# A time-mixing kernel: six batches transposed by three crossbar DMAs a group from overlapping rows, in place of one DMA a group in token order

## Chip, cores and metric

The kernel runs on one core of one Trainium2 chip. The metric is the device time of one execution in microseconds; the median of three runs of the kernel before is 199.16 us (198.97 to 199.38). The profile is of one execution more, and its times are counted from the start of that execution's span.

## The reference, cut to what matters

```python
x_prev[:, 1:, :] = x[:, :-1, :]                   # x: 16 batches x 2048 tokens x 256
xv = x * time_mix_v + x_prev * (1 - time_mix_v)
xr = x * time_mix_r + x_prev * (1 - time_mix_r)
v = xv @ value_weight
r = xr @ receptance_weight
out = (sigmoid(r) * v) @ output_weight            # float32, 16 x 2048 x 256
```

The key projection of the reference has no part in the output, and the kernel does not compute it.

## The kernel before

**Work on the engines.** The 32,768 tokens are cut into 64 units of 512 tokens, four a batch. The projections want the 256 channels on the partitions, so every batch of `x` is first transposed to bf16, as tile `xt`. The mix weights are folded into the projection weights, so that one mixed operand is `x + c * x_prev`: a scale of the previous tokens by `c` (`scale` L354 on DVE, `scale_pool` L364 on POOL, `scale_act` L652 on ACT) and an add of the tokens themselves (`add` L376 on DVE). Then PE does per unit four matmuls for r and four for v (`project`, L384), ACT the sigmoid of r (L672), DVE the product `z` with v (L711), PE eight matmuls with `z` as the stationary operand (`out_matmuls`, L416), and ACT the copy of that result to SBUF (L471). SP stores pairs of units, 1 MB each (`store`, L437), and at the end smaller pieces.

**Three ways to `xt`.** Batches 0 and 1 are transposed by PE unit by unit; batches 2 to 9 by PE from a tile in which partition p holds tokens 16p to 16p + 15. Their `xt` is in the *slot layout*: 17 slots of 128 columns, where column p of slot j + 1 is token 16p + j, and slot 0 holds slot 16 shifted by one column. A unit reads four slots for its tokens, and the same slots less one for the previous tokens (`tokens`, `slots`). Batches 10 to 15 take no PE transposes. POOL's DMAs (`load`, L162 and L158) cast them from float32 to bf16 into a DRAM tile `x_natural`, two groups of three batches, each batch behind 16 rows of zeros; then a crossbar DMA transpose on SP's queue (`by_dma`, L254) writes the group's `xt_both`. One DMA takes the whole group: 6192 rows (three times 16 + 2048) of 256 elements become 128 partitions of 2 x 6192 elements, in token order. A unit of batches 10 to 14 (`STAGED_PAIRS`) then picks runs of four columns out of 1024 consecutive tokens; a unit of batch 15 takes 512 consecutive tokens, and both give `z` an order of its own, which `out_matmuls` undoes by reading every second or fourth column.

**What sets the order around the change.** The program order is written out by hand, loop by loop (one loop a unit). The first group's transpose stands in the loop of unit 27, the second's in that of unit 39 (`T_AT`). Each waits by an added dependency until the last load of its group has landed, so that it does not run beside a load; the loads of batches 13 to 15 (`STAGE_AT`: loops 33 to 35, on POOL's queue) wait in turn for the first group's transpose. The stores of some units are held back so that SP's queue is free: `FIRST` sends two or one of them ahead of a transpose, `WAITING` sends two, then four, right behind it. SP's queue is served in order. The outputs lie in eleven buffers of 1 MB (seven `o_sb`, later also four `x_bf`), so stores may run late by some units without holding ACT.

Of the kernel before, what the change touches and what calls it, by code (L numbers as in the profile page):

```python
# [9 lines left out]
BF16 = mybir.dt.bfloat16  # L10
# [5 lines left out]
def kernel(  # L16
# [25 lines left out]
    nc = tc.nc  # L42

    B, S, D = x.shape
    P = 128
    KO = D // P
    J = S // P
    UJ = 4
    TU = UJ * P
# [5 lines left out]
    H = UJ // 2  # L55
# [7 lines left out]
    WAITING = {23: 27, 25: 27, 29: 39, 31: 39, 33: 39, 35: 39}  # L63
    ZEROS_AT = 12
    SINGLE = NU - 6
    STAGED_PAIRS = range(STAGED, B - 1)
    STAGE_AT = {33: 13, 34: 14, 35: 15}
    GROUPS = [(2, 3), (4, 5, 6), (7, 8, 9), (10, 11, 12), (13, 14, 15)]
    HALVED = (12, 15)
# [140 lines left out]
    def new_xt(b):  # L210
        if b >= BYUNIT:
            for group in GROUPS:
                if b != group[0]:
                    continue
                if b >= STAGED:
                    t = xtpool.tile([P, KO, len(group) * (PAD + S)], BF16, name="xt_both")
                    for k in range(len(group)):
                        xt[b + k] = t[:, :, k * (PAD + S) + PAD - 1 : (k + 1) * (PAD + S)]
                    xt_both[b] = t
                    return  # L220
                xt_both[b] = xtpool.tile([P, J + 1, KO, len(group), P], BF16, name="xt_both")
                for k in range(len(group)):
                    xt[b + k] = xt_both[b][:, :, :, k]
                    nc.gpsimd.memset(xt[b + k][:, 0, :, 0:1], 0.0)
            return
        xt[b] = consts.tile([P, UB * (UJ + 1), KO, P], BF16, name=f"xt_first{b}")
        (nc.vector if b == 0 else nc.gpsimd).memset(xt[b][:, 0, :, 0:1], 0.0)
# [23 lines left out]
    def by_dma(b, after):  # L251

        new_xt(b)
        op = nc.sync.dma_start_transpose(  # L254
            out=xt_both[b], in_=x_both[b].rearrange("b s d -> (b s) d")
        )
        tc.add_manual_dep(op.ins, after.ins.name, SYNC, reason="not beside a load")
        return op

    def transposes(i):  # L260

# [52 lines left out]
    def slots(piece, off=0):  # L314

        b, _, lo, hi = piece
        j = lo // P + (lo // TU if b < BYUNIT else 0) + off
        return slice(j, j + (hi - lo) // P)

    def by_unit(cols, lo, hi):  # L320

        assert hi - lo in (TU, 2 * TU)
        return cols if hi - lo > TU else cols[:, :, :, lo // TU % 2]

    def tokens(piece, off, ko=None):

        b, _, lo, hi = piece
        if b in STAGED_PAIRS:
            pair = lo // (2 * TU) * 2 * TU + off
            cols = xt[b][:, :, pair : pair + 2 * TU].rearrange("p k (q h i) -> p k q h i", h=2, i=UJ)  # L330
            cols = by_unit(cols, lo, hi)
            return cols if ko is None else cols[:, ko]
        if b < STAGED:
            cols = xt[b][:, slots(piece, off)]
        else:
            cols = xt[b][:, :, off + lo : off + hi].rearrange("p k (j c) -> p j k c", c=P)
        return cols if ko is None else cols[:, :, ko]

    def mixed(piece, ko=None):
        b, m, lo, hi = piece  # L340
        cols = mix[(b * S + lo) // (2 * TU)][:, m]
        if b in STAGED_PAIRS:
            cols = cols.rearrange("p j k c -> p (j k c)")
            cols = cols.rearrange("p (h k q i) -> p k q h i", h=2, k=KO, i=UJ)
            cols = by_unit(cols, lo, hi)
            return cols if ko is None else cols[:, ko]
        j = lo // P % (2 * UJ)
        cols = cols[:, j : j + (hi - lo) // P]
        return cols if ko is None else cols[:, :, ko]
# [53 lines left out]
                stop=(n == len(parts) - 1),  # L403
            )

    def out_matmuls(ps, z, b, jj, n, whole=False):

        if whole:
            slot = z.rearrange("p k (c j) -> p k j c", j=UJ)[:, :, jj : jj + n]
        else:  # L410
            cols = z[:, :, jj * P : (jj + n) * P]
            order = "p k (j c) -> p k j c" if b < STAGED else "p k (c j) -> p k j c"
            slot = cols.rearrange(order, j=n)
        for j in range(n):
            for ko in range(KO):
                nc.tensor.matmul(  # L416
                    out=ps[:, j, :],
                    lhsT=slot[:, ko, j],
                    rhs=wo_bf[:, ko, :],
                    start=(ko == 0),  # L420
                    stop=(ko == KO - 1),
                )

    def store(queue, b, lo, hi, after=None):
        src = o_sb[b, lo // (2 * UJ)]
        j = lo % (2 * UJ)
        src = src[:, j : j + hi - lo, :]
        if b < STAGED:
            dst = out[b].rearrange("(p j) d -> p j d", p=P)[:, lo:hi, :]
        elif b in STAGED_PAIRS:  # L430
            h = lo // (2 * UJ)
            dst = out[b, h * 2 * TU : (h + 1) * 2 * TU].rearrange("(p j) d -> p j d", p=P)[:, j : j + hi - lo]
        else:
            n = min(hi - lo, UJ)
            dst = out[b, lo * P : hi * P].rearrange("(e p j) d -> p e j d", p=P, j=n)
            src = src.rearrange("p (e j) d -> p e j d", j=n)
        op = queue.dma_start(out=dst, in_=src)  # L437
        if after is not None:
            tc.add_manual_dep(op.ins, after.ins.name, SYNC, reason="in turn with the last load")
# [16 lines left out]
    def output(g, z):  # L456
        b, e = divmod(g, UB)
        if e % 2 == 0:
            new_o(b, e // 2)
        o = o_sb[b, e // 2]  # L460
        j0 = e % 2 * UJ
        if g >= NU - 4:
            for h in range(2):
                ps = ps_t_pool.tile([P, H, D], FP32, name="ps_t")
                out_matmuls(ps, z, b, h * H, H, whole=True)
                nc.scalar.copy(out=o[:, j0 + h * H : j0 + (h + 1) * H, :], in_=ps)
            store(nc.sync, b, e * UJ, (e + 1) * UJ)
            return
        ps = ps_o_pool.tile([P, UJ, D], FP32, name="psum_o")
        out_matmuls(ps, z, b, 0, UJ)  # L470
        nc.scalar.copy(out=o[:, j0 : j0 + UJ, :], in_=ps)  # L471
        if b < BYUNIT:
            if e % 2 == 1:
                nc.sync.dma_start(
                    out=unit_rows(out, b, e - 1, 2), in_=o.rearrange("p (e j) d -> p e j d", j=UJ)
                )
        elif g >= SINGLE:
            store(nc.sync, b, e * UJ, (e + 1) * UJ)
        elif e % 2 == 1:
            pair = (b, (e - 1) * UJ, (e + 1) * UJ)  # L480
            if g in FIRST:
                firsts.setdefault(FIRST[g], []).append(pair)
            elif g in WAITING:
                kept.setdefault(WAITING[g], []).append(pair)
            else:
                store(nc.sync, *pair)
# [276 lines left out]
```

## Time and profile before

| | us |
|---|---|
| median of three runs | 199.16 |
| span of the profiled execution, first to last instruction | 197.1 |
| PE busy | 191.8 (97%) |
| DVE busy | 183.2 (93%) |
| ACT busy | 177.2 (90%) |
| POOL busy | 85.9 (44%) |
| first group's transpose: issued, landed 19.0 later | 95.12 |
| second group's transpose: issued, landed 15.2 later | 133.82 |
| last store issued | 193.77 |

The median of the runs is 2.06 us above the span of the profiled execution: what lies ahead of the first and behind the last instruction is not in the span. A row of the windows view gives a stretch, the busy time of each engine in it with the number of instructions, the granted clock of PE, the share of the 16 DMA engines' time that was in use (packets overlap, so a share can be over 1), and GB/s. A row of a timeline gives the start, the length, the engine, the line, the instruction and, in brackets, how long the engine was idle before and what ended that.

### The profile page before, as it was taken

To read this page: it belongs to the slowest core of one execution; us is meant where nothing else is said; L and a number is where in the kernel's file an instruction comes from. 1 tells how busy PE (TensorE), PEld (TensorE's weight loads), DVE (VectorE), ACT (ScalarE), POOL (GpSimd) and SP (SyncE) were. 2 spreads that over 40 slices of the span, in tenths; PEclk is the share of its full clock that TensorE was granted. 3 is DMA by queue.
4 is the path that set the end of the run, shared out by engine and by line. 5 is a ranking of instruction groups with operands and counts; after the bars stand their busy time and mean duration, and the time that the engine had idled before them with its cause. 6 is when DMAs were issued, how large, how long until landed. Compare 5 with 4: busy or idle time off the path is not lost.

```text
span 197.1 us, 3735 instructions
## 1 busy us (share of the span) xinstructions
PE 191.8 (97%) x1358; PEld 123.3 (63%) x1364; DVE 183.2 (93%) x286; ACT 177.2 (90%) x197; POOL 85.9 (44%) x117
## 2 busy tenths in 40 slices
PE   8999999999999999999999999999999999999992
PEld 3556676666666666666666666666666666666660
DVE  0999999999999999999999999999999999999962
ACT  3799899999999999999999999999999999999982
POOL 2745542443665635624334266444443444444200
PEclk9999999999999999999999999999999999999999
DMA  5999999999999999999999999999999999999875
GB/s 171 244 190 223 218 263 253 248 264 259 300 419 278 289 294 336 271 236 206 367 206 290 330 347 191 204 210 284 290 301 424 421 419 419 411 422 421 338 321 219
DMA packets 35465, 58.13 MB, mean 295 GB/s; under 512 B 26004, under 2 KB 27000, under 8 KB 30712
## 3 DMA queue, kind: packets, MB, share of 16 engines
q1 hardware_dynamic: 31792, 41.34, 59.8%
q0 software_dynamic: 3504, 16.44, 41.6%
q8 instruction: 10, 0.16, 0.3%
q10 hardware_dynamic: 152, 0.13, 0.2%
q14 instruction: 7, 0.06, 0.1%
HBM read 34.34 MB, written 39.90 MB: 377 GB/s over the span
## 4 chain that ended last, share of the span: by engine, by line
PE 93%; DMA 4%; issue 0%; SPq 0%; ACT 0%
PE psum_r L384 28%; PE psum_v L384 27%; PE psum_o L416 27%; PE ps_t L272 9%; DMA x_bf<-in_x_dram 2%; DMA w_f<-n_receptance_weight_dram 2%; PE ps_t L416 1%; SPq L174 0%; PE psum_v L416 0%; PE ps_t L384 0%; PE psum_r L416 0%; ACT x_bf L446 0%
## 5 line engine op out<-in xcount | busy, mean ns | idle before, releaser
L364 POOL TENSOR_SCALAR mix<-xt_both,c_sb 128x1024 bf16<-128x1024 bf16 (+1 forms) x55 | 61.1, 1110 | 85.6 <-DVE mix L376 82.4
L711 DVE TENSOR_TENSOR z_sb<-s_sb,psum_v 128x1024 bf16<-128x1024 bf16 (+1 forms) x64 | 76.7, 1200 | 2.2 <-PE psum_v L384 1.1
L376 DVE TENSOR_TENSOR mix<-mix,xt_both 128x1024 bf16<-128x1024 bf16 x112 | 76.8, 696 | 1.4
L384 PEld LDWEIGHTS <-w_bf 128*128 128x128 bf16 x512 | 48.5, 98 | 39.1 <-DVE mix L376 0.4
L672 ACT ACTIVATE s_sb<-psum_r 128x1024 bf16<-128x1024 f32 x63 | 65.3, 1036 | 6.2 <-PE psum_r L384 6.0
L384 PE MATMUL psum_v<-mix,w_bf 128*128 128x512 bf16 (+1 forms) x252 | 64.8, 378 | 0.2
L384 PE MATMUL psum_r<-mix,w_bf 128*128 128x512 bf16 x250 | 64.6, 379 | 0.2
L416 PE MATMUL psum_o<-wo_bf,z_sb 128*128 128x256 bf16 x486 | 63.2, 273 | 0.0
L416 PEld LDWEIGHTS <-z_sb 128*128 128x128 bf16 x512 | 51.9, 103 | 17.9 <-DVE z_sb L510 0.7
L471 ACT COPY o_sb<-psum_o 128x1024 f32<-128x1024 f32 x50 | 51.2, 1024 | 4.9 <-PE psum_o L416 4.9
L289 ACT COPY xt_both<-ps_t 128x1024 bf16<-128x1024 bf16 x32 | 32.9, 1039 | 0.0
L272 PEld LDWEIGHTS <-x_bf 128*128 128x128 bf16 x304 | 19.7, 98 | 8.6 <-DMA x_bf<-in_x_dram 1.1
L272 PE MATMUL ps_t<-ident,x_bf 128*128 128x128 bf16 x304 | 22.5, 219 | 0.3 <-DMA x_bf<-in_x_dram 0.3
L354 DVE TENSOR_SCALAR mix<-xt_both,c_sb 128x1024 bf16<-128x1024 bf16 (+1 forms) x47 | 21.3, 463 | 0.0
L652 ACT ACTIVATE mix<-xt_both,c_sb 128x1024 bf16<-128x1024 bf16 x14 | 16.3, 1163 | 0.0
L376 DVE TENSOR_TENSOR mix<-mix,xt_first 128x1024 bf16<-128x1024 bf16 x15 | 10.6, 714 | 0.1
L471 ACT COPY x_bf<-psum_o 128x1024 f32<-128x1024 f32 x10 | 10.2, 1016 | 0.0
L354 DVE TENSOR_SCALAR mix<-xt_first,c_sb 128x512 bf16<-128x512 bf16 x22 | 6.6, 352 | 0.2
L289 ACT COPY xt_first<-ps_t 128x1024 bf16<-128x1024 bf16 x6 | 6.1, 1042 | 0.2 <-PE ps_t L272 0.2
L557 POOL COPY xt_first<-xt_first 128x254 bf16<-128x254 bf16 x5 | 2.0, 392 | 7.2 <-DVE mix L376 5.7
L364 POOL TENSOR_SCALAR mix<-xt_first,c_sb 128x512 bf16<-128x512 bf16 x6 | 4.1, 685 | 1.5 <-DVE mix L376 1.0
L162 POOL DMA_DIRECT2D x_bf<-in_x_dram x8 | 4.7, 583 | 0.0
(68 smaller groups left out, 52.6 us busy)
## 6 DMA issues: line engine op xcount, KB each, us to landing
out_dram<-o_sb SPq DMA_DIRECT2D x25, 1024.0 KB, 11.6
x_bf<-in_x_dram POOLq DMA_DIRECT2D x8, 1024.0 KB, 14.8
x_natural<-in_x_dram POOLq DMA_DIRECT2D x4, 1024.0 KB, 11.8
out_dram<-x_bf SPq DMA_DIRECT2D x4, 1024.0 KB, 14.4
x_natural<-in_x_dram POOLq DMA_DIRECT2D x4, 512.0 KB, 12.6
out_dram<-x_bf SPq DMA_DIRECT2D x4, 512.0 KB, 4.2
x_bf<-in_x_dram POOLq DMA_DIRECT2D x6, 256.0 KB, 6.5
o_sb<-in_x_dram SPq DMA_DIRECT2D x4, 256.0 KB, 3.8
```

The costliest lines, as they stand in the source:

```text
L162: return nc.gpsimd.dma_start(out=x_bf[b], in_=rows(b), max_dma_last_dim=run)
L272: nc.tensor.transpose(out=ps[:, jj], in_=src[:, jj, ko * P : (ko + 1) * P], identity=idn)
L289: nc.scalar.copy(out=xt[b][:, j0 : j0 + UJ], in_=ps)
L354: nc.vector.tensor_scalar(out=mixed(piece, ko), in0=tokens(piece, 0, ko), scalar1=c_sb[:, m, ko : ko + 1], scalar2=None, op0=ALU.mult,)
L364: op = nc.gpsimd.tensor_scalar(out=mixed(piece, 1), in0=tokens(piece, 0, 1), scalar1=c_sb[:, m, 1:2], scalar2=1.0, op0=ALU.mult, op1=ALU.mult,
L376: return nc.vector.tensor_tensor(out=mixed(piece), in0=mixed(piece), in1=tokens(piece, 1), op=ALU.add)
L384: nc.tensor.matmul(out=ps[:, mo, :], lhsT=w_bf[:, m, ko, mo * P : (mo + 1) * P], rhs=mixed((b, m, e * TU + lo, e * TU + hi), ko), start=(k ...
L416: nc.tensor.matmul(out=ps[:, j, :], lhsT=slot[:, ko, j], rhs=wo_bf[:, ko, :], start=(ko == 0), stop=(ko == KO - 1),)
L471: nc.scalar.copy(out=o[:, j0 : j0 + UJ, :], in_=ps)
L652: nc.scalar.activation(out=mixed(piece, ko), in_=tokens(piece, 0, ko), func=ACT.Copy, scale=c_sb[:, m, ko : ko + 1],)
L672: nc.scalar.activation(out=s_sb, in_=ps_r, func=ACT.Sigmoid)
L711: nc.vector.tensor_tensor(out=z_sb[:, :, c : c + n], in0=s_sb[:, :, c : c + n], in1=ps_v[:, :, c : c + n], op=ALU.mult,)
```

## The change

For batches 10 to 15 the transposed tile now has the slot layout of batches 2 to 9. `by_dma` issues three transposes a group, one a batch. Each reads 128 rows of 4352 elements (17 tokens of 256) that start 16 tokens apart, so that neighbouring rows overlap by one token; the first token of the first row is the last row of zeros. Column group by column group they fill the 34 blocks of 128 columns (17 slots x 2 halves of the channels) of one batch. Slot 0 comes out shifted by the transpose itself. Token order, the four-column runs and the strided reads of `z` are gone, and the stores of all batches address the output as partition p, tokens 16p to 16p + 15.

```diff
@@ new_xt
-                if b >= STAGED:
-                    t = xtpool.tile([P, KO, len(group) * (PAD + S)], BF16, name="xt_both")
-                    for k in range(len(group)):
-                        xt[b + k] = t[:, :, k * (PAD + S) + PAD - 1 : (k + 1) * (PAD + S)]
-                    xt_both[b] = t
-                    return
                 xt_both[b] = xtpool.tile([P, J + 1, KO, len(group), P], BF16, name="xt_both")
                 for k in range(len(group)):
                     xt[b + k] = xt_both[b][:, :, :, k]
-                    nc.gpsimd.memset(xt[b + k][:, 0, :, 0:1], 0.0)
+                    if b < STAGED:
+                        nc.gpsimd.memset(xt[b + k][:, 0, :, 0:1], 0.0)
@@ by_dma
         new_xt(b)
-        op = nc.sync.dma_start_transpose(
-            out=xt_both[b], in_=x_both[b].rearrange("b s d -> (b s) d")
-        )
-        tc.add_manual_dep(op.ins, after.ins.name, SYNC, reason="not beside a load")
+        for k in range(len(next(group for group in GROUPS if group[0] == b))):
+            op = nc.sync.dma_start_transpose(
+                out=xt[b + k].rearrange("p j k c -> p (j k) c"), in_=shifted_rows(b, k)
+            )
+            tc.add_manual_dep(op.ins, after.ins.name, SYNC, reason="not beside a load")
         return op
+
+    def shifted_rows(b, k):
+
+        first = x_both[b][k, PAD - 1 : PAD - 1 + S].rearrange("(p j) d -> p (j d)", p=P)
+        steps = [list(step) for step in first.ap]
+        steps[-1][1] += D
+        return bass.AP(tensor=first.tensor, offset=first.offset, ap=steps)
@@ tokens
-        if b in STAGED_PAIRS:
-            pair = lo // (2 * TU) * 2 * TU + off
-            cols = xt[b][:, :, pair : pair + 2 * TU].rearrange("p k (q h i) -> p k q h i", h=2, i=UJ)
-            cols = by_unit(cols, lo, hi)
-            return cols if ko is None else cols[:, ko]
-        if b < STAGED:
-            cols = xt[b][:, slots(piece, off)]
-        else:
-            cols = xt[b][:, :, off + lo : off + hi].rearrange("p k (j c) -> p j k c", c=P)
+        cols = xt[b][:, slots(piece, off)]
...
@@ out_matmuls
-        if whole:
-            slot = z.rearrange("p k (c j) -> p k j c", j=UJ)[:, :, jj : jj + n]
-        else:
-            cols = z[:, :, jj * P : (jj + n) * P]
-            order = "p k (j c) -> p k j c" if b < STAGED else "p k (c j) -> p k j c"
-            slot = cols.rearrange(order, j=n)
+        slot = z[:, :, jj * P : (jj + n) * P].rearrange("p k (j c) -> p k j c", j=n)
@@ store
-        if b < STAGED:
-            dst = out[b].rearrange("(p j) d -> p j d", p=P)[:, lo:hi, :]
-        elif b in STAGED_PAIRS:
-            h = lo // (2 * UJ)
-            dst = out[b, h * 2 * TU : (h + 1) * 2 * TU].rearrange("(p j) d -> p j d", p=P)[:, j : j + hi - lo]
-        else:
-            n = min(hi - lo, UJ)
-            dst = out[b, lo * P : hi * P].rearrange("(e p j) d -> p e j d", p=P, j=n)
-            src = src.rearrange("p (e j) d -> p e j d", j=n)
+        dst = out[b].rearrange("(p j) d -> p j d", p=P)[:, lo:hi, :]
```

On SP's queue, from the last stores ahead of the first group's transpose to the first behind the second's, before (`o_sb` and `xt_both` numbers tell the buffers apart; DMAHW are the completions of DMAs of SP and ACT, DMASW those of POOL's):

```order
L437 DMA out_0_dram<-o_sb_1171 128x2048 [waits DMAHW2_49,Activation_49]
L254 DMA_TRANSPOSE xt_both_1401<-x_natural_136 128x2x6192 [waits DMASW5_49,DMASW1_49,DMASW6_49,DMASW0_49,DMAHW3_49,DVE_49,Pool_49]
L437 DMA out_0_dram<-o_sb_1255 128x2048 [waits DMAHW4_49,Activation_49]
L437 DMA out_0_dram<-o_sb_1333 128x2048 [waits DMAHW5_49,Activation_49]
L437 DMA out_0_dram<-o_sb_1416 128x2048 [waits DMAHW6_49,DMASW3_49,Activation_49]
L254 DMA_TRANSPOSE xt_both_1805<-x_natural_137 128x2x6192 [waits DMASW2_49,DMASW1_49,DMASW4_49,DVE_49,DMAHW7_49,Activation_49,Pool_49]
L437 DMA out_0_dram<-o_sb_1494 128x2048 [waits DMAHW0_49]
```

The same place now:

```order
L408 DMA out_0_dram<-o_sb_1171 128x2048 [waits DMAHW2_49,Activation_49]
L249 DMA_TRANSPOSE xt_both_1401<-x_natural_136 128x34x128 [waits DMASW5_49,DMASW0_49,DMAHW3_49,DVE_49,Pool_49]
L249 DMA_TRANSPOSE xt_both_1401<-x_natural_136 128x34x128 [waits DMAHW4_49,DMASW6_49]
L249 DMA_TRANSPOSE xt_both_1401<-x_natural_136 128x34x128 [waits DMAHW5_49,DMASW1_49]
L408 DMA out_0_dram<-o_sb_1255 128x2048 [waits DMAHW6_49,Activation_49]
L408 DMA out_0_dram<-o_sb_1333 128x2048 [waits DMAHW7_49,Activation_49]
L408 DMA out_0_dram<-o_sb_1418 128x2048 [waits DMAHW0_49,DMASW3_49,Activation_49]
L249 DMA_TRANSPOSE xt_both_1807<-x_natural_137 128x34x128 [waits DMASW2_49,DMASW1_49,DMASW4_49,DVE_49,DMAHW1_49,Activation_49,Pool_49]
L249 DMA_TRANSPOSE xt_both_1807<-x_natural_137 128x34x128 [waits DMAHW2_49,DMASW2_49]
L249 DMA_TRANSPOSE xt_both_1807<-x_natural_137 128x34x128 [waits DMAHW3_49]
L408 DMA out_0_dram<-o_sb_1496 128x2048 [waits DMAHW4_49]
```

Each transpose became three, one behind the other; the stores around them stand where they stood.

On POOL, the scales near the program's end, where the second group's tile is first read, before (each `mix` number is one pair of units, and two pairs make a batch):

```order
L364 TENSOR_SCALAR mix_201<-xt_both_1401,c_sb_134 128x128x2x4 [waits DVE_49]
L364 TENSOR_SCALAR mix_202<-xt_both_1805,c_sb_134 128x128x2x4 [waits DMAHW7_49,DVE_49,PE_49]
L364 TENSOR_SCALAR mix_202<-xt_both_1805,c_sb_134 128x128x2x4 [waits DVE_49]
L364 TENSOR_SCALAR mix_203<-xt_both_1805,c_sb_134 128x128x2x4 [waits DVE_49,PE_49]
L364 TENSOR_SCALAR mix_203<-xt_both_1805,c_sb_134 128x128x2x4 [waits DVE_49]
L364 TENSOR_SCALAR mix_204<-xt_both_1805,c_sb_134 128x128x2x4 [waits DVE_49,PE_49]
L364 TENSOR_SCALAR mix_204<-xt_both_1805,c_sb_134 128x128x2x4 [waits DVE_49]
L364 TENSOR_SCALAR mix_205<-xt_both_1805,c_sb_134 128x128x2x4 [waits DVE_49,PE_49]
L364 TENSOR_SCALAR mix_205<-xt_both_1805,c_sb_134 128x128x2x4 [waits DVE_49]
L364 TENSOR_SCALAR mix_206<-xt_both_1805,c_sb_134 128x8x128 [waits DVE_49,PE_49]
```

And now:

```order
L348 TENSOR_SCALAR mix_201<-xt_both_1401,c_sb_134 128x8x128 [waits DVE_49]
L348 TENSOR_SCALAR mix_202<-xt_both_1807,c_sb_134 128x8x128 [waits DMAHW1_49,DVE_49,PE_49]
L348 TENSOR_SCALAR mix_202<-xt_both_1807,c_sb_134 128x8x128 [waits DVE_49]
L348 TENSOR_SCALAR mix_203<-xt_both_1807,c_sb_134 128x8x128 [waits DVE_49,PE_49]
L348 TENSOR_SCALAR mix_203<-xt_both_1807,c_sb_134 128x8x128 [waits DVE_49]
L348 TENSOR_SCALAR mix_204<-xt_both_1807,c_sb_134 128x8x128 [waits DMAHW2_49,DVE_49,PE_49]
L348 TENSOR_SCALAR mix_204<-xt_both_1807,c_sb_134 128x8x128 [waits DVE_49]
L348 TENSOR_SCALAR mix_205<-xt_both_1807,c_sb_134 128x8x128 [waits DVE_49,PE_49]
L348 TENSOR_SCALAR mix_205<-xt_both_1807,c_sb_134 128x8x128 [waits DVE_49]
L348 TENSOR_SCALAR mix_206<-xt_both_1807,c_sb_134 128x8x128 [waits DMAHW3_49,DVE_49,PE_49]
```

The scales stand in the same order with another shape, and where the first scale of the group waited for the group's one DMA, the first scale of each batch now waits for that batch's own. On PE no instruction moved.

More of the change, by code (lines that the diff above doesn't have):

```diff
@@ L65 @@
     SINGLE = NU - 6
-    STAGED_PAIRS = range(STAGED, B - 1)
     STAGE_AT = {33: 13, 34: 14, 35: 15}
@@ L318, in slots @@
         return slice(j, j + (hi - lo) // P)
-    def by_unit(cols, lo, hi):
-        assert hi - lo in (TU, 2 * TU)
-        return cols if hi - lo > TU else cols[:, :, :, lo // TU % 2]
     def tokens(piece, off, ko=None):
         b, _, lo, hi = piece
-        if b in STAGED_PAIRS:
-            pair = lo // (2 * TU) * 2 * TU + off
-            cols = xt[b][:, :, pair : pair + 2 * TU].rearrange("p k (q h i) -> p k q h i", h=2, i=UJ)
-            cols = by_unit(cols, lo, hi)
-            return cols if ko is None else cols[:, ko]
-        if b < STAGED:
-            cols = xt[b][:, slots(piece, off)]
-        else:
-            cols = xt[b][:, :, off + lo : off + hi].rearrange("p k (j c) -> p j k c", c=P)
+        cols = xt[b][:, slots(piece, off)]
         return cols if ko is None else cols[:, :, ko]
@@ L341, in mixed @@
         cols = mix[(b * S + lo) // (2 * TU)][:, m]
[L342 to L346, printed above, removed]
         j = lo // P % (2 * UJ)
@@ L404, in project_unmixed, with out_matmuls @@
             )
-    def out_matmuls(ps, z, b, jj, n, whole=False):
-        if whole:
-            slot = z.rearrange("p k (c j) -> p k j c", j=UJ)[:, :, jj : jj + n]
-        else:
-            cols = z[:, :, jj * P : (jj + n) * P]
-            order = "p k (j c) -> p k j c" if b < STAGED else "p k (c j) -> p k j c"
-            slot = cols.rearrange(order, j=n)
+    def out_matmuls(ps, z, b, jj, n):
+        slot = z[:, :, jj * P : (jj + n) * P].rearrange("p k (j c) -> p k j c", j=n)
         for j in range(n):
@@ L464, in output @@
                 ps = ps_t_pool.tile([P, H, D], FP32, name="ps_t")
-                out_matmuls(ps, z, b, h * H, H, whole=True)
+                out_matmuls(ps, z, b, h * H, H)
                 nc.scalar.copy(out=o[:, j0 + h * H : j0 + (h + 1) * H, :], in_=ps)
```

## The prediction

> **What bounds the kernel now.** I read the page first, then the windows by stage, then SP's and POOL's timelines, then the DMA traffic around one transpose. The page, with the span, the engines' busy time and the chain that ended last:
>
> ```profile
> span 197.1 us, 3735 instructions
> PE 191.8 (97%) x1358; PEld 123.3 (63%) x1364; DVE 183.2 (93%) x286; ACT 177.2 (90%) x197; POOL 85.9 (44%) x117
> PE 93%; DMA 4%; issue 0%; SPq 0%; ACT 0%
> ```
>
> PE carries the chain. How much it idles between its first transpose and the last unit is in the windows (the heading names the columns; the last two numbers are the share of the DMA engines and GB/s):
>
> ```profile
> core 0: us, PE busy (x) PEld busy (x) DVE busy (x) ACT busy (x) POOL busy (x), PEclk, DMA share, GB/s
> 10.25:190.30 180.05, 179.69 (x1296) 116.56 (x1303) 176.17 (x263) 168.50 (x181) 80.92 (x102) 1.00 1.05 302
> 112.00:117.00 5.00, 5.00 (x33) 2.90 (x31) 4.90 (x8) 4.80 (x6) 2.46 (x3) 1.00 0.95 390
> 118.00:133.00 15.00, 14.95 (x94) 9.15 (x94) 14.97 (x21) 13.72 (x15) 7.76 (x8) 1.00 1.03 204
> 138.00:147.00 9.00, 8.89 (x55) 5.57 (x56) 8.98 (x14) 8.18 (x9) 3.47 (x4) 1.00 1.27 290
> 148.00:186.00 38.00, 37.84 (x235) 24.36 (x236) 37.87 (x52) 35.13 (x38) 16.20 (x15) 1.00 1.01 417
> 186.00:191.00 5.00, 5.00 (x37) 3.49 (x36) 3.73 (x6) 4.27 (x8) 0.00 (x0) 1.00 0.62 252
> 191.00:194.50 3.50, 2.33 (x18) 1.21 (x15) 1.87 (x4) 2.33 (x5) 0.00 (x0) 1.00 0.86 332
> ```
>
> In 180.05 us PE idles 180.05 - 179.69 = 0.36 us, at a granted clock of 1.00. So nothing that makes DVE, ACT or POOL faster can bring more than some tenths. The second thing to see is the last column but one. From 118 us on the DMA engines are full in every stage: loads (118 to 133), the second group's transpose (138 to 147), the backlog of stores (148 to 186). Only at 186 us, 5 to 8 us from the end, does the backlog clear. DMA is a second bound that stands just below PE.
>
> **Part one: operands, shapes, order.** The instructions of PE stay as they are; the scales and weight loads get the shape that batches 8 and 9 have already. The groups by shape for 116 to 128 us (slot layout) and then for 134 to 172 us (token order), mean ns of one before the second bar:
>
> ```profile
> L376 DVE TENSOR_TENSOR mix<-mix,xt_both 128x1024 bf16<-128x1024 bf16 x10 | 6.7, 688 | 0.0
> L364 POOL TENSOR_SCALAR mix<-xt_both,c_sb 128x1024 bf16<-128x1024 bf16 x5 | 5.6, 1115 | 5.3 <-DVE mix L376 5.3
> L416 PEld LDWEIGHTS <-z_sb 128*128 128x128 bf16 x40 | 3.9, 98 | 1.5
> ...
> L376 DVE TENSOR_TENSOR mix<-mix,xt_both 128x1024 bf16<-128x1024 bf16 x30 | 20.2, 690 | 0.0
> L364 POOL TENSOR_SCALAR mix<-xt_both,c_sb 128x1024 bf16<-128x1024 bf16 x15 | 16.8, 1122 | 22.0 <-DVE mix L376 20.7 <-PE psum_v L384 1.3
> L416 PEld LDWEIGHTS <-z_sb 128*128 128x128 bf16 x120 | 13.2, 114 | 3.3
> ```
>
> An add costs 690 ns against 688, a POOL scale 1122 against 1115, a weight load of `z` 114 against 98. The 16 ns of 192 weight loads (24 units by 8) are 3.1 us of PEld, but matmuls run over them: PE has no gap for them to fill beyond the 0.36 us. In the tail the weight loads themselves wait for DVE's `z`:
>
> ```profile
> 192.00 0.33 PEld L416 LDWEIGHTS <-z_sb 128*128 128x128 bf16 x4 [0.26 <-DVE z_sb L510]
> ```
> Gain: 0 to 0.4 us, and I take 0, since it would need all of PE's idle time to be of this kind. The stores of batches 10 to 15 now write pieces 16 KB apart in place of whole megabytes. In the backlog the first stores are of batches 7 to 9, which are written so already, the later ones of batches 10 and up:
>
> ```profile
> 150.00:155.00 5.00, 5.00 (x32) 3.22 (x31) 4.99 (x8) 4.59 (x6) 2.05 (x3) 1.00 1.02 424
> 165.00:170.00 5.00, 5.00 (x33) 3.24 (x32) 4.98 (x8) 4.59 (x6) 2.25 (x2) 1.00 1.01 421
> ```
>
> 424 against 421 GB/s: no price for 8 KB pieces. For the last stores' 1 to 4 KB pieces there is no such row; I take 0, within 0.1 us either way.
>
> **Part two: the transposes.** SP's queue, and the landing of the two transposes:
>
> ```profile
> 95.12 15.38 SPq L254 DMA_TRANSPOSE xt_both<-x_natural  x1
> 110.61 20.99 SPq L437 DMA_DIRECT2D out_dram<-o_sb  x3
> 133.82 12.33 SPq L254 DMA_TRANSPOSE xt_both<-x_natural  x1
> 146.20 3.41 SPq L437 DMA_DIRECT2D out_dram<-o_sb  x4
> ...
> DMA to landing us min/median/max: 15.2/17.1/19.0
> ...
> DMA packets 10200, 2.61 MB, mean 290 GB/s; under 512 B 10200, under 2 KB 10200, under 8 KB 10200
> ```
>
> The last row is the DMA traffic of 138 to 147 us: 10200 packets in 9 us, 256 B each, at 290 GB/s, and nothing else in flight. So the rate is the transpose's own. A group was 6192 rows of 512 B, 3.17 MB: 10.93 us. It becomes 3 x 128 rows of 8704 B, 3.34 MB: 11.52 us at the same rate. **Size: +0.59 us a group, +1.18 us both.**
>
> The two added boundaries in each group have no row in this trace; two neighbours bound them. Traffic of 133 to 149 us in 40 slices of 0.4 us:
>
> ```profile
> GB/s 369 451 430 410 389 311 205 154 116 36 222 291 288 291 291 288 291 291 288 291 291 288 291 291 288 291 291 288 291 291 288 291 291 288 291 291 447 532 389 369
> ```
>
> From stores to a transpose there is a hole: the five slices from 135.4 us lack 85 + 136 + 174 + 254 + 68 = 717 of 290 GB/s each, 0.29 MB, 0.99 us of transposing. From the transpose to stores there is none: SP is done with it at 133.82 + 12.33 = 146.15 us, the store behind is issued at 146.20, and in the slice at 147.4 the one's data give way to the other's. A second transpose behind a first would also be issued some 1.3 us before the first one's data end, and no store packet is left that delays some of the 16 engines more than others. So the boundary is nearest to the row without a hole; but the first data of a transpose may need a little longer than a store's, so below 0 it cannot go. Bounds 0 and 0.99 us, value 0.15, times four: **+0.6 us** (0 to 4.0). Should the 128 short source rows, 8 KB apart, read more slowly, that is a rival below; the value here is the same rate. **Sum: the DMA work between 95 and 149 us grows by 1.18 + 0.6 = 1.8 us.**
>
> **What the 1.8 us are worth.** The DMAs of the two groups form one line: transpose one, loads of batches 13 to 15 (held until it lands), transpose two (held until they land), backlog. What is added is spent where the DMA engines are idle: 5 x 0.05 = 0.25 us at 112 to 117, 5 x 0.38 = 1.9 us at 186 to 191, 3.5 x 0.14 = 0.5 us at 191 to 194.5. Together 2.6 us. 1.8 fit; the last store starts when its copy is done, as before. If the added time is D, the end moves by D - 2.6 where that is positive. It moves by more than 0.2% (0.4 us, about what a measurement of this kernel can tell from no change) from D = 3.0.
>
> **Who waits for a later landing.** POOL's queue:
>
> ```profile
> 113.47 1.12 POOL L364 TENSOR_SCALAR mix<-xt_both,c_sb 128x1024 bf16<-128x1024 bf16 x1 [2.33 <-DVE mix L376]
> 114.64 0.56 POOL L162 DMA_DIRECT2D x_natural<-in_x_dram  x1
> 116.22 1.11 POOL L364 TENSOR_SCALAR mix<-xt_both,c_sb 128x1024 bf16<-128x1024 bf16 x1 [1.02 <-DVE mix L376]
> 123.82 1.12 POOL L364 TENSOR_SCALAR mix<-xt_both,c_sb 128x1024 bf16<-128x1024 bf16 x1 [1.31 <-DVE mix L376]
> 154.99 1.12 POOL L364 TENSOR_SCALAR mix<-xt_both,c_sb 128x1024 bf16<-128x1024 bf16 x1 [1.29 <-PE psum_v L384]
> ```
>
> The load at 114.64 waits for the first group's landing at 95.12 + 19.0 = 114.1 and reached its place at 114.59; the scale behind it idles 1.02 us more. With +0.9 us the group lands at 115.0 and the scale at 116.22 still starts in time; from about +1.5 us it would start late. The first readers of the two groups stand at 123.82 and 154.99, 9.7 and 6.0 us after the landings (the second 133.82 + 15.2 = 149.0). Now each batch waits for its own third, so that slack only grows. The stores behind the transposes leave SP 1 us later; their buffers, eleven for a pair of units each, are due again only several pairs later.
>
> **The rivals.** *A hole at each boundary.* Each of the three transposes starts as the one behind stores did. For it: the only start in the trace has a hole. Against it: there it goes with packets of stores still in flight on some engines. At 0.75 us, D = 1.18 + 3.0 = 4.2, the end 1.6 us later: 200.7; at 0.99, 201.7. It decides from (3.0 - 1.18) / 4 = 0.46 us.
>
> *The short rows read more slowly.* A packet reads 256 B. Before, neighbouring rows lay 512 B apart and 8 KB were read in one piece; now neighbouring rows lie 8 KB apart, and the same row is read again only 128 packets later. For it: the loads show a DMA that moves only 204 GB/s while the engines are full. Against it: the flat 288 to 291 GB/s of the slices look like a pace of the engines, not of the memory. Halfway between 290 and 204, at 247 GB/s, a group takes 13.5 us, D = 2 x 2.6 + 0.6 = 5.8, the end 3.2 us later: 202.3; at 204, some 208. It decides from 275 GB/s.
>
> The Trainium skill, page "DMA: Bandwidth & Descriptors", section "Latency and other measured facts", gives crossbar transposes 350 to 400 GB/s for contiguous sources and 261 with a middle dimension that is not contiguous, a loss of about 30%. This trace has 290 for a contiguous source, so the page's first figure does not hold here; whether its loss does, no run here shows yet. By 261 GB/s as it stands a group would take 12.8 us, D would be 4.4, and the end 200.9 us, by an estimate from that page. The same page's section on crossbar transposes names nothing against sources whose rows overlap.
>
> *POOL held at the load.* If transpose one lands over 3 us late, the scales behind the load come late, DVE's adds after them, and PE idles: over 203 us. It needs one of the two rivals above at its upper end.
>
> *Faster.* PE's idle 0.36 us is all that shorter scales and weight loads could give: 198.8 at best.
>
> **How the numbers follow.** The forecast, absorbed: 0.50, at the median of before, 199.2 (the profiled span of 197.1 plus the 2.06 us outside it). Hole at the boundaries: 0.20, 199.6 to 201.7. Slower reading: 0.20, 199.6 to 208. POOL held: 0.04. Faster: 0.06. The range reaches down to 198.8 and up to 201.4: that leaves out half of the faster case, half of the slower reading, a little of the holes, and POOL held, under 0.2 together. Chances: faster 0.06, same 0.50, slower 0.44.
>
> **What would show it.** Right: the transposes at about 290 GB/s with no dip between three, a group's data over in 11.5 to 12 us, PE idle still under 0.5 us from 10 to 190 us, the backlog clearing near 188 and the DMA share of 186 to 191 nearer to 1. Wrong: dips at the boundaries, a rate under 275, or a DMA share of 1 up to the last store. PE gaps between 115 and 125 us would show POOL held.

## The result, and the profile after

The changed kernel takes 207.46 us (median of four runs, 207.08 to 208.35) against 199.15 us (198.97 to 199.38): a ratio of 1.0417 [1.0378, 1.0457], 8.3 us slower. The forecast was 199.2 us, with a range up to 201.4. Times of traces are those of one profiled execution each; its span was 205.4 us, against 197.1 before. One of the ten runs of number 5 below took 1148.26 us, for a reason not known, and is not in its ratio; every other run counts.

The page, with the span, the engines and the chain that ended last, by engine and then by line:

```profile
span 205.4 us, 3751 instructions
PE 191.9 (93%) x1364; PEld 120.7 (59%) x1364; DVE 183.1 (89%) x286; ACT 177.3 (86%) x197; POOL 86.1 (42%) x117
PE 77%; DMA 6%; DVE 4%; SPq 4%; issue 2%; POOL 2%; ACT 1%; DVEq 0%; POOLq 0%
PE psum_v L368 23%; PE psum_r L368 22%; PE psum_o L395 22%; PE ps_t L274 7%; DMA xt_both<-x_natural 4%; SPq L249 3%; DMA w_f<-n_receptance_weight_dram 2%; DVE mix L360 2%; POOL mix L348 1%; DVE z_sb L682 1%; PE ps_t L395 1%; DVE mix L338 1%; PE psum_r L382 1%; ACT xt_first L284 1%; SPq L173 0%
```

No engine has more to do: PE is busy for 191.9 us, against 191.8. But the transposes stand on the chain now (DMA `xt_both` 4%, SP's queue at L249 3%), and before they did not. The windows, columns as before:

```profile
120.00:125.00 5.00, 3.13 (x20) 1.80 (x19) 4.57 (x7) 3.35 (x4) 4.02 (x6) 1.00 1.04 288
130.00:190.00 60.00, 60.00 (x373) 36.30 (x371) 59.71 (x82) 55.51 (x60) 25.01 (x23) 1.00 1.01 332
186.00:191.00 5.00, 5.00 (x33) 3.05 (x32) 4.97 (x7) 4.77 (x7) 1.12 (x1) 1.00 1.02 421
191.00:196.00 5.00, 4.94 (x37) 3.15 (x35) 3.16 (x7) 4.09 (x9) 0.00 (x0) 1.00 1.01 414
196.00:204.00 8.00, 0.00 (x0) 0.00 (x0) 0.07 (x1) 0.35 (x1) 0.00 (x0) 0.66 0.85 325
```

Two things differ. PE has one hole, 1.9 us between 120 and 125. And the backlog of stores, which cleared at 186 us before (a DMA share of 0.62 at 186 to 191), now fills the DMA engines to the end: 1.02, 1.01, and still 0.85 in the last 8 us, in which PE does nothing. The last copy to SBUF starts at 195.97 us; the last store lands at 204.2, where it landed at 196.1 before.

Where the backlog was delayed is seen in SP's timeline (three merged transposes a row) and in the slices of the DMA traffic, first 97 to 120 us (0.575 us a slice), then 140 to 160 us (0.5 us a slice):

```profile
95.70 20.41 SPq L249 DMA_TRANSPOSE xt_both<-x_natural  x3
116.21 20.53 SPq L408 DMA_DIRECT2D out_dram<-o_sb  x3
140.26 15.34 SPq L249 DMA_TRANSPOSE xt_both<-x_natural  x3
```
```profile
GB/s 427 328 299 256 228 214 147 176 191 154 290 290 288 292 83 158 100 91 121 289 289 290 291 258 74 245 18 83 295 94 5 41 291 291 289 477 442 299 399 456
GB/s 344 148 16 88 141 79 126 260 289 290 291 289 292 105 52 220 198 115 173 291 290 289 292 285 88 124 139 186 280 288 291 290 291 391 419 426 328 492 410 393
```

Between their starts the transposes run at the same flat rate as before, 288 to 292 GB/s, but for one stop in the first group (number 2). Each of the three starts with a dip, though. The second of the second group: 105, 52, 220, 198, 115, 173 lack 877 of 6 x 290, and 877 / 290 x 0.5 us = 1.5 us. By the trace's packets (256 B each, 1133 a microsecond at the steady rate) the data of the first group, from the first packet to the last, take 17.72 us, from 99.92 to 117.64, against 12.37 before (99.72 to 112.09); those of the second 15.59 us, from 141.58 to 157.17, against 12.38 (135.30 to 147.68).

PE's hole comes through POOL. The rows of POOL, DVE and PE:

```profile
118.67 0.56 POOL L161 DMA_DIRECT2D x_natural<-in_x_dram  x1 [3.73 <-DMA xt_both<-x_natural]
119.27 1.13 POOL L348 TENSOR_SCALAR mix<-xt_both,c_sb 128x1024 bf16<-128x1024 bf16 x1
120.43 0.69 DVE L360 TENSOR_TENSOR mix<-mix,xt_both 128x1024 bf16<-128x1024 bf16 x1 [2.22 <-POOL mix L348]
122.30 1.02 PE L368 MATMUL psum_v<-mix,w_bf 128*128 128x512 bf16 x4 [1.87 <-DVE z_sb L682]
```

The load waits for the last of the three landings (118.14 us, against 114.1) and holds POOL's queue; the scale behind it starts at 119.27 instead of 116.22, DVE's add waits 2.22 us for it, and PE 1.87 us for the `z` behind that.

### The profile page after: what moved, and what is told of

It is laid out like the page before. It is cut to its first block, busy times and chain, and to the rows that moved or that the text cites. A ratio compares the mean times of both kernels' runs of the same rounds, so it can differ in the third digit from the quotient of the medians.

```text
span 205.4 us, 3751 instructions
## 1 busy us (share of the span) xinstructions
PE 191.9 (93%) x1364; PEld 120.7 (59%) x1364; DVE 183.1 (89%) x286; ACT 177.3 (86%) x197; POOL 86.1 (42%) x117
## 4 chain that ended last, share of the span: by engine, by line
PE 77%; DMA 6%; DVE 4%; SPq 4%; issue 2%; POOL 2%; ACT 1%; DVEq 0%; POOLq 0%
PE psum_v L368 23%; PE psum_r L368 22%; PE psum_o L395 22%; PE ps_t L274 7%; DMA xt_both<-x_natural 4%; SPq L249 3%; DMA w_f<-n_receptance_weight_dram 2%; DVE mix L360 2%; POOL mix L348 1%; DVE z_sb L682 1%; PE ps_t L395 1%; DVE mix L338 1%; PE psum_r L382 1%; ACT xt_first L284 1%; SPq L173 0%
## 5 line engine op out<-in xcount | busy, mean ns | idle before, releaser
L395 PEld LDWEIGHTS <-z_sb 128*128 128x128 bf16 x512 | 49.8, 98 | 19.7 <-DVE z_sb L481 0.7
```

What stands on the lines that cost most here:

```text
L395: nc.tensor.matmul(out=ps[:, j, :], lhsT=slot[:, ko, j], rhs=wo_bf[:, ko, :], start=(ko == 0), stop=(ko == KO - 1),)
```

## The experiments

Two questions were asked: what lengthens the transposes, and which of the two consequences, the late stores or PE's hole, sets the time. Below, the loss of a transpose or a group is the time of its data less its packets at 1133 a microsecond, so 0 means the steady rate from the first packet to the last; what a start loses is what has been lost by the time the rate is flat. Each ratio is to runs of the kernel before that were made along with the run, with medians of 199.11 to 199.35 us.

**1. Three DMAs a group, in token order (`e1_three_token_order`).** The kernel before, with its one transpose cut into one a batch; rows, layout and bytes stay.

```diff
-        op = nc.sync.dma_start_transpose(
-            out=xt_both[b], in_=x_both[b].rearrange("b s d -> (b s) d")
-        )
+        for k in range(len(next(group for group in GROUPS if group[0] == b))):
+            op = nc.sync.dma_start_transpose(
+                out=xt_both[b][:, :, k * (PAD + S) : (k + 1) * (PAD + S)], in_=x_both[b][k]
+            )
```

> The kernel before with its one transpose a group cut into three, one a batch (2064 rows each), token order and all else as before. Theory S (each crossbar DMA has a slow start of its own, whatever it reads): two more starts a group cost what the changed kernel's profile lost beyond its size, (17.7 - 12.4) + (15.6 - 12.4) = 8.5 us less 1.2 us of size, over four boundaries, some 1.8 us each, so about 7.3 us more DMA work, of which some 2 us are absorbed at the end: 204 to 206 us, with a dip in the 256-byte traffic at each third. Theory R (the short rows 8 KB apart read slowly at first, the number of DMAs does not matter): 199.2 us within 0.4, no dips at the thirds.

Measured: 202.0 us (201.39 to 202.33), ratio 1.0125 [1.008, 1.017]. Traffic at 97 to 120 us, and the last windows:

```profile
GB/s 356 385 242 256 211 183 58 276 290 290 290 291 182 178 183 284 290 287 290 285 143 85 57 288 290 289 291 290 368 427 427 442 442 399 370 413 456 200 57 214
```
```profile
186.00:191.00 5.00, 5.00 (x33) 3.24 (x32) 4.55 (x7) 4.40 (x7) 0.00 (x0) 1.00 1.01 409
191.00:196.00 5.00, 3.15 (x25) 1.94 (x23) 1.86 (x4) 3.01 (x6) 0.00 (x0) 1.00 0.98 382
196.00:204.00 8.00, 0.00 (x0) 0.00 (x0) 0.00 (x0) 0.00 (x0) 0.00 (x0) 0.76 0.08 29
```

Neither theory alone: starting again costs 0.7 to 1.2 us each (182, 178, 183 is the second start, 143, 85, 57 the third), 3.8 us for the four, and the data of the groups take 13.86 and 14.03 us. The time is 2.8 us longer, of the changed kernel's 8.3. The data of the second group end 3.3 us later than before, in the changed kernel 9.5 us. Of the 6.2 us between the two, about 3 are dearer starts (all six counted), 1.2 the size and 1.4 a fetch of instructions (number 2); most of the rest lies between the groups. The span is 2.5 us longer, so only 0.8 us was absorbed in this execution, where the prediction had up to 2.6.

**2. One DMA a group, from the overlapping rows (`e2_one_strided`).** The other part alone: 400 rows (`ROWS`) over all three batches in one transpose. It also transposes rows between the batches (13,600 packets instead of 12,384, 12.00 us at the steady rate), and writes a small block of zeros behind the last batch and one column a batch.

```diff
-        for k in range(len(next(group for group in GROUPS if group[0] == b))):
-            op = nc.sync.dma_start_transpose(
-                out=xt[b + k].rearrange("p j k c -> p (j k) c"), in_=shifted_rows(b, k)
-            )
+        op = nc.sync.dma_start_transpose(
+            out=xt_both[b].rearrange("p j k c -> p (j k) c"), in_=shifted_rows(b)
+        )
...
+        steps[0][1] = ROWS
```

> The changed kernel with one transpose a group over 400 rows 16 tokens apart (386 are needed; the rest are padding rows, zeroed by one small DMA a group), slot layout as in the changed kernel. Size by the 290 GB/s of the trace: 400 x 8704 B = 3.48 MB, 12.0 us against 10.9 before, so 2.1 us more for both. Theory S: one start a group as before, no dips inside, all of the 2.1 us absorbed: 199.0 to 199.8 us. Theory R: the reads are as far apart as in the changed kernel and the slow stretches stay: 205 us or more.

Measured: 202.81 us (202.04 to 204.78), ratio 1.0184 [1.0113, 1.0256]. Neither theory's time came: it lies between the two, and the profiled execution is the slowest of the four. The steady rate from these rows is 289 to 291 GB/s: they are not read more slowly in the run. The one start of each group loses 1.70 and 1.79 us, against 1.20 and 1.34 before. Over all of their data the groups lose 3.06 and 2.71 us (1.44 and 1.45 before), since each has one stop more, which is no start. In the first group it is the last 1.4 us of the data, behind a fetch of 16 KB of instructions at 114.74 us. In the second it stands in the middle of the run. Traffic at 148 to 153 us, 0.125 us a slice, and the queue that stands beside it:

```profile
GB/s 291 287 287 291 291 295 289 293 287 287 289 293 295 289 285 295 287 289 293 350 270 268 274 102 27 12 8 8 8 6 92 289 289 295 289 293 289 289 283 295
q14 instruction: 1, 0.01, 0.5%
```

A fetch of 8 KB of instructions starts at 150.44 us, one packet, and so on one of the 16 DMA engines; 0.4 us later the transpose stands almost still on all of them: 0.9 us lost. The same is found in the changed kernel, at 111 to 119 us (0.2 us a slice), where 16 KB were fetched at 113.60:

```profile
GB/s 20 200 289 262 140 14 4 17 8 93 278 253 355 248 102 14 0 4 9 10 9 101 292 288 297 287 291 287 292 288 297 287 287 684 655 0 655 655 0 655
q8 instruction: 1, 0.02, 0.7%
```

The first stop, from 111.8 us, is the start of the third transpose; the second, from 113.8 to 115.2, lies in the middle of it and loses 1.4 us. In numbers 3, 6 and 9, which also have three transposes a group, a 16 KB fetch falls into the run of the first group's third transpose too, and 1.5 to 1.6 us are lost.

**3. The loads of the second group one unit later (`e3_loads_later`).** The changed kernel; POOL's scale no longer stands behind a load that waits.

```diff
-    STAGE_AT = {33: 13, 34: 14, 35: 15}
+    STAGE_AT = {34: 13, 35: 14, 36: 15}
```

> The changed kernel with the loads of batches 13 to 15 one loop later in the program, so that POOL reaches the first of them when the first group has nearly landed. In the changed kernel's profile POOL sat 3.7 us at that load and PE idled some 1.9 us at 120 to 125 us. Theory D (the end is set by the DMA engines, which are full up to the last store): PE's gap goes or shrinks below 0.5 us and the time stays within 1 us of 207.5. Theory W (the wait on POOL is what the time was lost to): 205.5 us or less.

Measured: 206.94 us (206.15 to 207.26), ratio 1.0387 [1.0337, 1.0437], which can't be told from the changed kernel's [1.0378, 1.0457]. The windows:

```profile
112.00:130.00 18.00, 18.00 (x112) 10.75 (x110) 17.86 (x26) 16.64 (x18) 9.34 (x11) 1.00 1.10 257
191.00:196.00 5.00, 2.81 (x22) 1.63 (x20) 1.86 (x4) 2.80 (x6) 0.00 (x0) 1.00 1.01 413
196.00:204.00 8.00, 0.00 (x0) 0.00 (x0) 0.00 (x0) 0.00 (x0) 0.00 (x0) 0.63 0.73 277
```

PE's hole is gone (18.00 of 18.00 us) and the time stays: the end is set by the stores, and PE's 1.9 us lie beside them.

**4. Six DMAs a group (`e4_six`).** The changed kernel with each transpose cut in two at slot 16: many long and short starts.

```diff
+            for lo, hi in ((0, UB * 2), (UB * 2, J + 1)):
+                op = nc.sync.dma_start_transpose(
+                    out=xt[b + k][:, lo:hi].rearrange("p j k c -> p (j k) c"),
+                    in_=shifted_rows(b, k)[:, lo * D : hi * D],
...
```

> The changed kernel with each batch's transpose cut into two (16 and 18 blocks of 128 columns), six a group, same rows, same bytes. Theory S: six more starts at some 1.8 us each, 11 us more DMA work with nothing left to absorb it, and POOL held longer at its load: 216 to 222 us. Theory R: the same reads in the same order, 207 to 209 us.

Measured: 209.6 us (one run). Neither theory's time came, and the second is nearer. Data of 17.98 and 18.05 us; the twelve starts lose 0.3 to 1.5 us, 0.95 on average. So the count of starts is not all: twice as many add 0.3 and 2.5 us to the groups (1.5 of the 2.5 are a fetch in the run, at 157.57 us), not the 4 to 5 us that three more starts at the changed kernel's price would add. Where DMAs are short (1.8 and 2.0 us of data each at the steady rate), a start costs less. Why was not found out.

**5 and 6. The changed kernel with less to store (`e5_later_less`, `e6_less`).** The four held stores behind the second group's transposes are left out, 4.2 MB of output that is not written; at 417 GB/s that is 10 us of DMA work, more than was added. Number 5 has the later loads of number 3 as well, number 6 has not.

```diff
-            for pair in kept.pop(g, []):
+            for pair in kept.pop(g, []) if g < CROSS else []:
```

> The kernel of the run before last (loads one loop later, no gap of PE left) with the four stores behind the second group's transposes left out: 4.2 MB of output are not written, some 10 us of DMA work at 417 GB/s. Theory D (the end is set by the line of DMA work alone): the line now ends before PE does, and the time is PE's own, 199.0 to 199.8 us. Theory P (something else in the changed kernel, its operands or its stores, slows PE or the tail): over 200.5 us.

> The changed kernel, loads where they were, with the same four stores left out. With the line of DMA work out of the way the wait on POOL should show alone. Theory D: 1.9 us above the run without that wait, 200.9 to 201.8 us. Theory W (the wait on POOL is most of the loss): 204 us or more. If the wait is made up for later: 199.5 us.

Measured: number 5 takes 199.37 us (nine of the ten runs 198.80 to 200.45), ratio 1.0006 [0.9984, 1.0029]; number 6 takes 201.23 us (200.75 to 201.69), ratio 1.0087 [1.0054, 1.0121]. The windows of number 5:

```profile
112.00:130.00 18.00, 18.00 (x112) 10.73 (x111) 17.87 (x26) 16.68 (x18) 9.30 (x11) 1.00 1.08 263
130.00:190.00 60.00, 60.00 (x375) 36.47 (x374) 59.38 (x82) 55.22 (x59) 24.10 (x22) 1.00 1.00 317
186.00:191.00 5.00, 5.00 (x35) 3.16 (x33) 4.25 (x6) 4.27 (x8) 0.00 (x0) 1.00 0.62 247
```

With room in the DMA line and no hole in PE, the changed kernel takes what the kernel before takes: the two together are the whole of the loss. What would only lengthen the line of DMA work, a slower store for instance, number 5 can't show, since it has 10 us less of that work. For this there are the rows of the changed kernel above: its stores of 186 to 196 us, which have the new addresses, move 421 and 414 GB/s, against 417 in the backlog of before. The hole alone is worth 201.23 - 199.37 = 1.9 us. The waits of number 6 at 112 to 130 us (who waited for whom, sum, times, longest) show it as the same chain as in the changed kernel:

```profile
POOL x_natural L161 <- DMA xt_both<-x_natural: 3.3, 1, 3.3
DVE mix L360 <- POOL mix L348: 1.8, 1, 1.8
PE psum_v L368 <- DVE z_sb L682: 1.4, 1, 1.4
```

**7. A store between the transposes (`e7_stores_between`).** The changed kernel, with two of the held stores put between the three transposes. If a start is slow because the transpose before is still draining, ordinary packets could fill it.

```diff
+            if k < 2:
+                store(nc.sync, *between.pop(0))
...
-            last_t = by_dma(T_AT[g], whole)
+            last_t = by_dma(T_AT[g], whole, kept.get(g, []))
```

> The changed kernel with one held store of 1 MB behind the first and one behind the second transpose of each group, in place of all of them behind the third; the same work in another order. Theory F (at a start the DMA engines lack descriptors, and a store's data fill the hole): of four starts at some 1.4 us most are filled, 202 to 204 us. Theory K (a transpose needs all 16 engines in step, and store packets put them out of step, so that a start behind a store costs as much or more): 207 us or above.

Measured: 209.35 us (208.54 to 210.25), ratio 1.0496 [1.0447, 1.0544]. Traffic at 97 to 120 us:

```profile
GB/s 413 342 299 299 232 155 106 132 78 199 289 290 290 290 376 442 328 356 85 199 187 150 232 237 289 289 289 291 401 399 356 328 100 228 202 155 258 261 289 289
```

The store passes at 328 to 442 GB/s, and behind it the transpose starts with the same dip (85, 199, 187, 150, 232, 237: 1.3 us). Less the two stores (2.5 us each at 417 GB/s) the groups lose 5.2 and 5.6 us, 1.7 to 1.9 us a start (with a 16 KB fetch at 142.10 us in the second group's first start). The slow start belongs to the transpose that starts, and a store ahead of it does not make it cheaper. The time by itself would not show this. With the stores in between, the third transpose lands later still, POOL waits 7.5 us at its load, and PE has a hole of 5.6 us:

```profile
112.00:130.00 18.00, 12.40 (x66) 6.65 (x65) 11.60 (x18) 10.27 (x12) 6.58 (x8) 0.81 0.96 215
```

**8. The first transpose one unit later (`e8_before_one_later`).** The kernel before; it was to move the transpose, and the stores held around it, against the instruction fetch.

```diff
-    T_AT = {27: 10, 39: 13}
...
+    T_AT = {28: 10, 39: 13}
...
```

> The kernel before with its first transpose one loop (3 us) later. In its profile a 16 KB fetch of instructions came at 111.84 us, as that transpose's data ended; in four other profiles here one came while a transpose ran, and its 256-byte traffic then fell to a tenth for 1.2 to 1.6 us. Theory I (the fetch stops the transpose): the fetch, at about 112 us, falls into the data, and they take 13.5 to 14.2 us in place of 12.4. Against it: 12.2 to 12.7 us, wherever the fetch falls. In either case the line of DMA work starts some 2 to 3 us later, so 200 to 203 us.

Measured: 200.7 us (one run). The transpose hardly moved (issued at 95.66 us, 95.12 before); the fetch did, to 116.62 us, outside the data. So it doesn't say what it was made for, and why it takes 200.7 us was not found out. It does show a first group without a fetch (11.84 us of data, 0.5 us less than before), and a second with a fetch of 16 KB at 136.46 us, within its start (13.09 us, 0.7 us more).

**9. Rows 8704 B apart (`e9_pitch`).** The changed kernel, with a DRAM tile in which every row of 17 tokens has its own place, so that no rows overlap and they no longer lie 8192 B apart. One more load a batch (64 KB) writes the repeated tokens.

```diff
-        x_both[group[0]] = dpool.tile([len(group), PAD + S, D], BF16, name="x_natural")
+        x_both[group[0]] = dpool.tile([len(group), P + 1, J + 1, D], BF16, name="x_natural")
...
+        return x_both[b][k, :P].rearrange("p j d -> p (j d)")
```

> The changed kernel with its DRAM tile cast into rows of 17 tokens each (8704 B apart, none overlapping) in place of rows 8192 B apart that overlap by one token; the token ahead of each row comes by one small load more a batch, 64 KB. The transposes read the same number of bytes in the same order. In the profiles so far a second or third start cost 1.0 to 1.8 us with rows 8 KB apart (mean 1.4) and 0.7 to 1.2 with whole batches in one piece (mean 0.95). Theory Q (the power-of-two distance makes a start slower): the starts come down to about 0.95 us, some 2.5 us less in both groups, 205 to 206 us with the small loads. Theory N (short rows far apart are slower at a start, whatever the distance): starts of 1.4 us as before, 207 to 209 us.

Measured: 206.1 us (205.82 to 206.95), ratio 1.0362 [1.0335, 1.0389]: by the medians 1.4 us less than the changed kernel, in spite of the added loads, though the intervals overlap a little (1.0378 to 1.0389). Traffic at 138 to 160 us, 0.55 us a slice:

```profile
GB/s 209 216 439 417 357 432 292 160 105 133 288 290 290 290 290 222 85 141 148 289 290 290 290 290 220 107 92 95 290 290 289 290 290 471 275 462 477 372 358 477
```

The starts are shorter: 1.04 to 1.25 us, 1.14 on average over the five without a fetch, between the 0.95 of theory Q and the 1.4 of theory N. So the way the rows lie matters, but this is a part of what the rows of the change cost. The edit changed two things at once, the distance and the overlap; which of them helps is not shown.

**10. The instruction fetch moved (`e10_fetch_earlier`).** The kernel before, with its first warm-up on PE replaced by more and smaller matmuls. PE's program gets longer at its head, and so the fetches of 16 KB come earlier in the work.

```diff
-    warm_up(WARM)
+    ps_warm = ps_t_pool.tile([P, TU], FP32, name="ps_t")
+    for _ in range(48):
+        nc.tensor.matmul(
+            out=ps_warm[:, :64], lhsT=ones, rhs=wide[:, :64], start=True, stop=True
+        )
```

> The kernel before with its first warm-up on PE (six matmuls of 512 columns and one of 128) replaced by 48 matmuls of 64 columns: 82 PE instructions more at the very start. If the 16 KB fetches are PE's, they come some 5 to 6 us earlier against the rest, the one at 111.84 us then in the middle of the first group's data. Theory I (a fetch stops a transpose): those data take 13.5 to 14.2 us in place of 12.4, and the time rises by 0.3 to 1.5 us. Against it: 12.2 to 12.7 us with a fetch in the middle, and the time within 0.5 us of before. Where no fetch falls into the data the run says nothing.

Measured: 199.77 us (199.15 to 200.28, ten runs), ratio 1.0024 [1.0001, 1.0047]. The fetch came at 110.81 us in place of 111.84, one microsecond earlier and not 5 to 6. Traffic at 109 to 114 us, first of the kernel before, then of this one, 0.125 us a slice:

```profile
GB/s 293 291 287 291 287 291 293 293 291 283 295 287 291 293 293 291 283 289 293 291 293 293 1244 18 80 918 0 131 852 66 852 66 328 721 66 852 66 524 524 66
q8 instruction: 1, 0.02, 1.4%
```
```profile
GB/s 285 293 287 291 295 291 283 293 293 287 291 295 291 283 414 274 268 272 41 18 2 0 0 2 8 8 10 8 10 12 254 295 293 289 291 293 287 285 293 295
q8 instruction: 1, 0.02, 1.5%
```

Before, the fetch fell on the moment in which the stores took over. A microsecond earlier it falls into the run, and the transpose stands for 1.4 us; the data of this group take 14.11 us in place of 12.37 (its start, too, loses more, 1.66 us against 1.20). The second group had a 16 KB fetch at 135.14 us, just ahead of its first packet; now its fetches come at 149.08 us, with its last packets, and it takes 12.03 us in place of 12.38. The time moved by only 0.24% [0.01%, 0.47%].

## Why the prediction was wrong

**The step that failed** is the boundary term of part two: 0.15 us, four times, 0.6 us in all, with bounds of 0 and 0.99. Measured, the added starts cost 1.8, 1.6, 1.5 and 1.1 us, 6.0 us in all, above the upper bound of 4.0. (The third of the first group lost 3.0 us, of which some 1.4 are the fetch; the two run into each other.) The reason given was half right. The next transpose was indeed issued before the data of the one ahead ended (109.54 us, flat rate until 110.7), and no store was in flight. But that a hole needs stores in flight was wrong: number 7 shows the same dip behind a store, number 1 behind a transpose. The trace of before had the right row: its start from stores to a transpose, which the prediction measured at 0.99 us and then set aside for the row of the other direction, a transpose giving way to stores. That is another operation's start. The one row of a transpose starting was the one to take. Its 0.99 us lies within the 0.7 to 1.2 that number 1 measured with the rows of before. (Counted by packets this start lost 1.34 us and the first group's 1.20; the slices of the traffic also count bytes of the last stores.) The rival of a hole at each boundary, with a chance of 0.20, had this mechanism; its highest price, 201.7 us, was still too low.

**What was missing** is that the rows of the change make a start dearer. Means of starts without a 16 KB fetch inside: 0.92 us from contiguous tokens (number 1, 0.7 to 1.2), 1.14 from rows 8704 B apart (number 9, 1.04 to 1.25), 1.4 from rows 8192 B apart (the changed kernel and number 3, 1.1 to 1.8; in number 5 one lost 2.15). The groups do overlap: the whole-group starts from contiguous tokens in before and in numbers 8 and 10 lost 0.77 to 1.66 us. Also missing was the fetch of instructions, 1.4 us. Before, the 16 KB fetch of the first group came at 111.84 us, as its data ended, and that of the second at 135.14, just ahead of its first packet; the longer data of the first group reach over the one.

The sum, from the profiled executions, up to the end of the second group's data:

| | predicted, us | measured, us |
|---|---|---|
| first start later | 0 | 0.2 |
| size, both groups | 1.18 | 1.2 |
| four added starts | 0.6 | 6.0 |
| fetch within the first group | – | 1.4 |
| from the first group's data to the second's, longer | 0 | 0.7 |
| D | 1.8 | 9.5 |
| absorbed (D less the end) | 1.8 of up to 2.6 | 1.2 |
| end later | 0 | 8.3 |

**What the D is worth** was right as a rule and wrong in size. Above the slack the end moves with D, and number 5 shows that nothing else moves it but PE's hole. The slack was too large: by the profiled executions 0.8 us was absorbed in number 1 and 1.2 us in the changed kernel, of 2.6 us. The prediction counted the idle share of the 16 engines as if the added work could fill all of it. In number 1 it did: the share is 1.01 and 0.98 from 186 to 196 us, and 8 x 0.08 = 0.6 us of work are left behind that. The end moved by 2.5 us all the same. Why is not shown; no run was made on that alone.

**POOL held at the load** was named with its price and its place, and came: the landing is 4.0 us later, the scale 3.05 us, and PE stands 1.9 us. The prediction had it from 3 us on, over 203 us. The price was too high: alone it makes 201.2 us (number 6). In the changed kernel it is worth nothing (number 3), because the stores end later still. It was a second bound that the first one hides, not an addition to it.

**Slower reading** was wrong in the form given, a lower rate throughout: 288 to 292 GB/s from all these rows. The Trainium skill, page "DMA: Bandwidth & Descriptors", section "Latency and other measured facts", has 261 GB/s for a source whose middle dimension is not contiguous, a loss of about 30%. In the steady run no such loss is seen here, and its 350 to 400 GB/s for contiguous sources are not reached either (290). The mean over a whole group fell from 256 GB/s (3.17 MB in 12.37 us) to 189 and 214 GB/s (3.34 MB in 17.72 and 15.59 us), 16 to 26% less. All of that lies in the starts and the fetch.

**The fetch.** The Trainium skill, page "Runtime: NRT & Kernel Launch", section "Instruction fetch mechanics", says that a sequencer fetches its instructions in blocks of 16 KB over a DMA queue of its own, mostly hidden. The fetches of 16 KB are in the trace, and PE did not wait for them (it idles 0.36 us of 180 before); but what they did to a transpose in flight was not hidden (numbers 2 and 10).

**Right** were the steady rate of 290 GB/s, the size term, and part one: shapes, operands and stores in another order cost nothing (number 5 comes out at 199.37 us with them, and the stores keep their rate). The first readers of the two groups never waited for the transposes.

**Open:** why a transpose of the changed kernel starts at less than half of its rate for 2 to 2.6 us (1.1 to 1.8 us lost), why rows 8 KB apart make this worse, why short transposes start more cheaply (number 4), why 0.7 us more pass between the first group's data and the second's, and why a fetch on one engine stops all 16. None of the kernels was faster than the one before, which is bound by PE.

## What to carry to other kernels

A crossbar transpose has a price for starting, here mostly 0.7 to 1.8 us, so in a line of full DMA engines one large transpose beats three, and a simpler layout has to earn that back. To price a new boundary, take the row of the same operation starting, in the same direction, however much its surroundings seem to excuse it. Slack read from a mean DMA share was more than twice what was absorbed here, and a second wait that the first one hides needs an experiment of its own.

## What was not expected of the hardware

- A fetch of instructions (16 KB in 0.9 to 1.4 us, 8 KB in 0.3 to 0.7 us), one packet on one DMA engine, brings a running transpose on all 16 to a stand: 1.4 us lost in the changed kernel and in number 10, 0.9 us for 8 KB in number 2.
- How the source rows lie changes the start of a transpose (1.14 us at 8704 B apart without overlap, 1.4 us at 8192 B apart with it) and not its steady rate.
- Ordinary stores between two transposes move at 328 to 442 GB/s and don't shorten the start behind them (1.7 to 1.9 us).
